# Seeding a PSUM bank by ScalarE for block product 2, and one more two-part group per layer, in a two-layer trunk

## The chip, the cores and the metric

The kernel runs on one core of one Trainium2 chip. The metric is the device time of one execution in microseconds; for the kernel before, the median of three runs is 967.45 us (967.29 to 968.33). The profile is of one further execution of the same program.

## The reference

The reference is a decoder trunk with two layers over 512 positions of 1,024 channels, batch 1, everything in float32. Each layer adds a mixer and then a gated convolutional FFN to the residual `h`. The change is in the FFNs alone:

```python
def gated_conv_ffn(x, w_gate, w_up, conv_w, conv_b, w_down):
    g = jnp.einsum('bsd,df->bsf', x, w_gate)
    g = causal_dwconv3(g, conv_w) + conv_b
    up = jnp.einsum('bsd,df->bsf', x, w_up)
    return jnp.einsum('bsf,fd->bsd', jax.nn.silu(g) * up, w_down)
...
        hn = rms_norm(h, norm_ffn[layer])
        h = h + gated_conv_ffn(hn, w_ffn_gate[layer], w_ffn_up[layer], conv_ffn[layer],
                               b_conv_ffn[layer], w_ffn_down[layer])
```

`w_gate` and `w_up` are 1,024 x 2,816 and `w_down` is 2,816 x 1,024; `causal_dwconv3` is a width-3 convolution along the positions.

## The kernel before

**Arithmetic.** A float32 product is computed from a high and a low part of each operand, both in the type fp32r: high times high, high times low, low times high. The high part is a ScalarE copy that rounds (`halves`, L831, or `parts`), the low part what is left, by a subtraction on VectorE (L832). Some low parts are made otherwise: ScalarE writes the negated rounded value (L144, L862) and a DMA on POOL's queue adds the source onto it (L146, L863).

**Groups.** The 2,816 hidden columns are 22 tiles of 128. In each layer the first two tiles are computed plainly (`direct`). The other twenty are ten groups of two tiles, f = 2, 4, ..., 20. `products` computes a group, for the gate (key "g") and for the up projection (key "u"), each as one 2 x 2 block product over two halves of the contraction, two column tiles and two halves of the positions, with seven block products instead of eight (Strassen-Winograd). So a group has 14 block products, of 128 columns of weights by 256 positions each, over four slices of 128 of the contraction.

**Narrow and wide.** A block product runs in one of two forms in `multiply`. The narrow form (L680) has three matmuls of 256 positions for each slice, twelve in all. The wide form (`both`, L670) gives one matmul the high and the low part of the positions side by side, 512 columns, for the high weights, and one of 256 columns for the low weights, eight matmuls in all. Its result lies in both halves of a PSUM bank, and the halves have to be added. `FIRST_WIDE` and `in_both` say which groups are wide. In layer 0, u is narrow before group 6; in group 6 g is wide and u wide in products 2, 5 and 3 alone; from group 8 on all is wide. In layer 1 it is the same two tiles earlier: mixed in group 4, all wide from group 6.

**Banks.** There are seven PSUM banks of 512 columns (`mm_bank`), taken in turn. By `BANK`, products 1, 6, 7 and 4 of one key accumulate in one bank "a" one after another, without clearing; products 5 and 3 share a bank "e"; product 2 has a bank "b" of its own. After a product, `after` reads the bank's running sum: a ScalarE copy to SBUF (L919, into `pads`, whose tiles are named rows, for g, or into `kept` for u), and VectorE adds of 256 columns (L907), one for each further half and each destination that the product contributes to (`onto`: product 2 is added where product 1 was put). A later product of the same bank can only be written once these reads are done.

**Order.** In `products` the fourteen block products are listed in an order by hand: g1, u1, g2, g5, g6, u5, u6, g7, u2, u7, g3, u3, g4, u4. After g3 and g4 the row is multiplied by the norm's factor (L931), convolved (`conv`: ScalarE L714, VectorE L716) and put through SiLU (L724); the products with u follow (L939 to L946). Between two groups stand matmuls of the down projection (`project` in layer 0, tiles d; `half_down` in layer 1, tiles dn), whose results VectorE adds to `h` (L317) or `y` (L1334).

**Preparation.** While one group runs, `prepare` makes the weights of the next: sums and differences of weight blocks on VectorE (s12g, s34g, s12u, s34u; L852 to L875) and their high and low parts (whi_..., wlo_...). In these groups the low parts of s12g, s34g and of the raw weights raw_g and raw_u go by the accumulating DMA, those of s12u and s34u by VectorE. A scheduler orders the instructions of each engine from the dependences, with priorities by the order of the source; each engine then runs its own list in order.

Of the kernel before, what the change touches and what calls it, by code (L numbers as in the profile page):

```python
# [31 lines left out]
def tile_trunk(ctx: ExitStack, tc: tile.TileContext, x, norm_mix, norm_ffn, final_norm,  # L32
# [3 lines left out]
    nc = tc.nc  # L36
# [9 lines left out]
    def mm_bank(name):  # L46
        return ps_mm.tile([P, 512], F32, tag="mm", name=name)
# [242 lines left out]
    def padded_tile():  # L290
        turn[0] += 1
        return padded[turn[0] % NPADDED]
# [352 lines left out]
    HALF = S // 2  # L645
# [1 line left out]
    PAIRS = [k for i in range(NP) for k in (i, i + NP)]  # L647

    FIRST_BY_DMA = 4
    FIRST_WIDE = ({"g": 6, "u": 8}, {"g": 4, "u": 6})  # L650

    BANK = {1: "a", 6: "a", 7: "a", 4: "a", 5: "e", 3: "e", 2: "b"}

# [37 lines left out]
    class Ffn:  # L691
# [195 lines left out]
        def products(self, f, stat):  # L887

            layer, ap, n = self.layer, self.ap, f"{self.layer}_{f}"
            banks = {"g": {}, "u": {}}  # L890
            kept = ap.tile([P, 3, HALF], F32, tag="kept", bufs=1, name=f"kept{n}")
            pads = [padded_tile() for _ in range(2)]
            lo, hi = slice(2, 2 + HALF), slice(2 + HALF, 2 + S)
            dst = {("g", 1): pads[0][:, lo], ("g", 6): pads[0][:, hi], ("g", 7): pads[1][:, hi],
                   ("g", 4): pads[1][:, lo]}
            dst.update({("u", product): kept[:, i, :] for i, product in enumerate((1, 6, 7))})
            onto = {2: 1, 7: 7, 3: 6}
            s = {}

            def in_both(key, product):  # L900
                first = FIRST_WIDE[layer]
                return f >= first[key] or f == first["g"] and product in (2, 5, 3)

            def add(d, bank, halves):
                ins = None
                for half in halves:
                    ins = nc.vector.tensor_tensor(d, bank[:, half * HALF : (half + 1) * HALF], d,  # L907
                                                  ALU.add)
                return ins

            def after(key, product, bank):
                halves = range(1 + in_both(key, product))
                if product in onto:
                    ins = add(dst[key, onto[product]], bank, halves)
                    if product == 7:
                        self.added[key] = ins
                elif (key, product) != ("u", 4):
                    d = dst[key, 7 if product == 5 else product]
                    nc.scalar.copy(d, bank[:, :HALF])  # L919
                    add(d, bank, halves[1:])  # L920

            for i, (key, product) in enumerate((
                    ("g", 1), ("u", 1), ("g", 2), ("g", 5), ("g", 6), ("u", 5), ("u", 6),
                    ("g", 7), ("u", 2), ("u", 7), ("g", 3), ("u", 3), ("g", 4), ("u", 4))):
                bank = self.multiply(banks[key], f"{key}{n}", product, stat[key, product],
                                     in_both(key, product), i % 2 == 1)
                after(key, product, bank)
                if (key, product) in (("g", 4), ("g", 3)):
                    j = product == 4
                    row = pads[j][:, 2:]  # L930
                    nc.vector.tensor_tensor(row, row, self.r, ALU.mult)  # L931
                    s[j] = self.silu(self.conv(pads[j], f + j), f + j)
                    if j and layer == 0:
                        nc.vector.tensor_tensor(s[1], s[1], self.r, ALU.mult)
            if layer == 0:
                nc.vector.tensor_tensor(kept[:, :2, :], kept[:, :2, :],
                                        self.r.rearrange("p (a b) -> p a b", a=2), ALU.mult)
            s0 = s[0].rearrange("p (a b) -> p a b", a=2)
            nc.vector.tensor_tensor(s0, kept[:, :2, :], s0, ALU.mult)  # L939
            nc.vector.tensor_tensor(s[1][:, HALF:], kept[:, 2, :], s[1][:, HALF:], ALU.mult)  # L940
            last = bank[:, :HALF]
            if in_both("u", 4):
                last = kept[:, 0, :]
                nc.scalar.copy(last, bank[:, :HALF])
                add(last, bank, (1,))
            nc.vector.tensor_tensor(s[1][:, :HALF], last, s[1][:, :HALF], ALU.mult)  # L946
            return [(f + 1, s[1]), (f, s[0])]
# [35 lines left out]
    def ffn0(norm):  # L983
        nonlocal prm1
        with tc.tile_pool(name="f0", bufs=1) as ap:
            def sums(kp):
                return [ap.tile([P, 2, HALF], F32R, name=f"t{i}_{kp}") for i in (2, 3)]

            ffn = Ffn(0, prm0, norm, ap, sums)
            def half_down(a, b, half):  # L990
                project(f"d0_{a}", w_ffn_down[0], ffn.acts, list(range(a, b)), None,
                        halves=(half,), tail=0)

            ffn.split_acts(ffn.steps(half_down))
            prm1 = params1(lambda ins: behind(ins, last_matmul[0]))
            nxt = Norm("m1", lambda k: prm1("mix", k))
            project("d0_last", w_ffn_down[0], ffn.acts, list(range(NF - 4, NF)), nxt)
            return nxt
# [547 lines left out]
    n = mixer0()  # L1546
    n = ffn0(n)
    n = mixer1(n)
# [31 lines left out]
```

## Time and profile before

| | |
|---|---|
| median of three runs | 967.45 us |
| the profiled execution | 968.03 us |
| its span | 966.3 us |
| TensorE matmul busy | 957.6 us (99%) |
| VectorE busy | 847.0 us (88%) |
| ScalarE busy | 620.7 us (64%) |
| GpSimd busy | 161.6 us (17%) |
| 256-column add, L907 | 0.42 us |
| 256-column copy, L919 | 0.36 us |

The page names the engines PE (TensorE's matmuls), PEld (its weight loads), DVE (VectorE), ACT (ScalarE), POOL (GpSimd) and SP (SyncE). A row of a timeline gives start, duration, engine, line, operation, output tile <- input tiles, and the shape; consecutive alike instructions are one row (x4). Ends of matmuls are modelled, so that the distance of two starts is the better measure of a matmul. Tiles g_12a and the like are the bank "a" of g's group 12. L numbers of the profile before are lines of the kernel before.

### The profile page before, as it was taken

The page shows a single profiled execution, that of the slowest core. Times are in us where ns is not written, and L with a number is a line of the kernel's source. Part 1 is how long each engine was busy: PE and PEld are TensorE (multiplying, and loading weights), DVE is VectorE, ACT ScalarE, POOL GpSimd, SP SyncE. Part 2 cuts the span into 40 slices and gives each one's busy share as a digit, 9 for nine tenths or more (in the row PEclk, how much of TensorE's full clock was granted, in tenths as well). Part 3 has the DMA queues.
Part 4 walks back from the last instruction along what each step waited for, and adds up shares of the span by engine and source line. Part 5 has one row for each costly group of instructions (what it writes and reads, how often), then busy time and mean ns, then how long its engine had stood idle before and what let it go on. Part 6 is the DMA issues. An engine that isn't in the chain of part 4 may idle for free.

```text
span 966.3 us, 14230 instructions
## 1 busy us (share of the span) xinstructions
PE 957.6 (99%) x5152; PEld 827.2 (86%) x5152; DVE 847.0 (88%) x1435; ACT 620.7 (64%) x940; POOL 161.6 (17%) x183
## 2 busy tenths in 40 slices
PE   9999999999999999999999999999999999999996
PEld 7888898998888888888888888989888888888885
DVE  5887988989899998998878689889998989889898
ACT  4624657766575565765487847787665667646775
POOL 2142224111011010110311002321111011100123
PEclk9999999999999999999999999999999999999999
DMA  7342345677777677774352323467767777667775
GB/s 253 134 151 87 66 135 128 170 188 188 175 174 174 154 174 196 164 184 132 131 153 87 109 88 88 140 137 182 183 150 191 196 175 174 177 151 196 196 152 142
DMA packets 95825, 150.45 MB, mean 156 GB/s; under 512 B 5284, under 2 KB 61580, under 8 KB 95756
## 3 DMA queue, kind: packets, MB, share of 16 engines
q1 hardware_dynamic: 78284, 98.69, 32.1%
q0 software_dynamic: 15696, 49.03, 28.1%
q10 hardware_dynamic: 1776, 1.84, 0.6%
q8 instruction: 40, 0.66, 0.3%
q14 instruction: 29, 0.24, 0.1%
HBM read 98.42 MB, written 2.10 MB: 104 GB/s over the span
## 4 chain that ended last, share of the span: by engine, by line
PE 99%; DVE 1%; issue 0%; POOLq 0%; DVEq 0%; POOL 0%; ACT 0%
PE d L159 3%; PE d L160 3%; PE dn L159 3%; PE dn L160 3%; PE dn L161 3%; PE d L161 3%; PE vu_a L1129 2%; PE gu L159 2%; PE gu L161 2%; PE gu L160 2%; PE u_2a L680 1%; PE g_2a L680 1%; PE u_4a L680 1%; PE u_20a L670 1%; PE u_18a L670 1%; PE u_12a L670 1%
## 5 line engine op out<-in xcount | busy, mean ns | idle before, releaser
L146 POOL DMA_DIRECT2D wlo_g<-raw_g x20 | 17.2, 860 | 310.0 <-DVE kept L907 142.2
L716 DVE SCALAR_TENSOR_TENSOR c<-rows,prm,c 128x512 f32<-128x512 f32 x88 | 65.4, 745 | 1.5 <-ACT c L714 1.5
L159 PE MATMUL d<-a_hi,whi_d 128*128 128x512 f32 x144 | 56.1, 389 | 0.0
L159 PE MATMUL dn<-whi_dn,a_hi 128*128 128x512 f32 x144 | 56.1, 389 | 0.0
L160 PE MATMUL d<-a_lo,whi_d 128*128 128x512 f32 x144 | 56.1, 389 | 0.0
L160 PE MATMUL dn<-wlo_dn,a_hi 128*128 128x512 f32 x144 | 56.0, 389 | 0.0
L161 PE MATMUL d<-a_hi,wlo_d 128*128 128x512 f32 x144 | 56.0, 389 | 0.0
L161 PE MATMUL dn<-whi_dn,a_lo 128*128 128x512 f32 x144 | 56.0, 389 | 0.0
L831 ACT ACTIVATE whi_a<-raw_g 128x512 fp32r<-128x512 f32 x20 | 12.6, 630 | 61.0 <-PE g_14e L670 8.5
L714 ACT ACTIVATE c<-rows,prm 128x512 f32<-128x512 f32 x44 | 31.4, 716 | 16.7 <-DVE rows L931 16.7
L1334 DVE SCALAR_TENSOR_TENSOR y<-dn,small,y 128x512 f32<-128x512 f32 x40 | 28.0, 749 | 7.8 <-PE dn L161 7.7
L724 ACT ACTIVATE s<-c,prm 128x512 f32<-128x512 f32 x44 | 31.4, 717 | 3.6 <-DVE c L716 3.6
L204 ACT ACTIVATE hg<-h,prm 128x512 fp32r<-128x512 f32 x24 | 17.3, 719 | 23.5 <-DVE h L317 17.0
L155 DVE TENSOR_TENSOR wlo_dn<-raw_dn,whi_dn 128x1024 fp32r<-128x1024 f32 x18 | 22.0, 1223 | 11.5 <-ACT whi_dn L154 11.5
L161 PEld LDWEIGHTS d<-a_hi,wlo_d 128*128 128x128 f32 x144 | 27.0, 188 | 5.7
L161 PEld LDWEIGHTS dn<-whi_dn,a_lo 128*128 128x128 f32 x144 | 27.0, 188 | 5.6
L160 PEld LDWEIGHTS dn<-wlo_dn,a_hi 128*128 128x128 f32 x144 | 27.0, 188 | 5.6
L159 PEld LDWEIGHTS dn<-whi_dn,a_hi 128*128 128x128 f32 x144 | 27.0, 188 | 5.6
L160 PEld LDWEIGHTS d<-a_lo,whi_d 128*128 128x128 f32 x144 | 27.1, 188 | 5.5
L159 PEld LDWEIGHTS d<-a_hi,whi_d 128*128 128x128 f32 x144 | 27.0, 188 | 5.5
L268 ACT ACTIVATE a_hi<-s 128x512 fp32r<-128x512 f32 x40 | 24.7, 625 | 10.5 <-PE d L161 9.4
L144 ACT ACTIVATE wlo_g<-raw_g 128x1024 fp32r<-128x1024 f32 x20 | 20.9, 1047 | 16.3 <-PE g_2e L680 7.6
(1271 smaller groups left out, 3377.7 us busy)
## 6 DMA issues: line engine op xcount, KB each, us to landing
raw_g<-in_w_ffn_gate_dram SPq DMA_DIRECT2D x40, 512.0 KB, 4.0
raw_u<-in_w_ffn_up_dram SPq DMA_DIRECT2D x40, 512.0 KB, 4.5
raw_dn<-in_w_ffn_down_dram SPq DMA_DIRECT2D x22, 512.0 KB, 4.7
wlo_g<-raw_g POOLq DMA_DIRECT2D x20, 512.0 KB, 4.5
wlo_u<-raw_u POOLq DMA_DIRECT2D x20, 512.0 KB, 6.0
raw_d<-in_w_ffn_down_dram SPq DMA_DIRECT2D x18, 512.0 KB, 4.1
wlo_s12g<-s12g POOLq DMA_DIRECT2D x18, 512.0 KB, 5.3
wlo_s34g<-s34g POOLq DMA_DIRECT2D x18, 512.0 KB, 5.2
```

The lines of the kernel that those rows point to most:

```text
L144: first = nc.scalar.activation(lo, raw, AF.Copy, scale=-1.0)
L155: behind(nc.vector.tensor_tensor(lo, raw, hi.bitcast(F32), ALU.subtract), after[0])
L159: nc.tensor.matmul(ps, lhs[0], rhs[0], start=start, stop=False)
L160: nc.tensor.matmul(ps, lhs[0], rhs[1], start=False, stop=False)
L161: nc.tensor.matmul(ps, lhs[1], rhs[0], start=False, stop=stop)
L268: nc.scalar.activation(hi, src, AF.Copy, scale=scale)
L670: last_matmul[0] = nc.tensor.matmul(ps if low else banks[at], left(kp)[low], right(kp)[0] if low else both(kp), start=first, stop=kp == NP ...
L680: nc.tensor.matmul(ps, l, r, start=first, stop=end, skip_group_check=True)
L714: nc.scalar.activation(c, t[:, 0:S], AF.Copy, scale=prm("cf", ft))
L716: self.last_conv = nc.vector.scalar_tensor_tensor(c, t[:, i : S + i], prm("cf", i * NF + ft), c, op0=ALU.mult, op1=ALU.add)
L724: self.last_silu = nc.scalar.activation(s, c, AF.Silu, bias=self.prm("bf", ft))
L1334: return nc.vector.scalar_tensor_tensor(dst, ps, ffn.cols[:, t : t + 1], dst, op0=ALU.mult, op1=ALU.add)
```

## The change

Two settings and the order of one product change, and `after` gets a second way.

- `FIRST_WIDE` moves one group earlier in both layers: the mixed group is now layer 0's group 4 and layer 1's group 2, and all groups behind are wide.
- From group 6 in layer 0 and group 4 in layer 1 (`FIRST_SEEDED`), product 1 is no longer read out to SBUF. Instead ScalarE copies its bank "a", both halves, to a new bank "b" (`seed`), and product 2 accumulates onto that bank, since `multiply` finds it there and does not clear it. Product 2's bank, now the sum of products 1 and 2, is then copied to product 1's destination and its second half added.
- g's copy is issued right after product 1 of g, u's after product 5 of u and ahead of that product's own copy.
- In the list of products, g5 now stands before g2.

```diff
@@ -647,7 +647,8 @@
-    FIRST_WIDE = ({"g": 6, "u": 8}, {"g": 4, "u": 6})
+    FIRST_WIDE = ({"g": 4, "u": 6}, {"g": 2, "u": 4})
+    FIRST_SEEDED = (6, 4)
@@ -908,9 +909,25 @@
+            def seeded(key):
+                return f >= FIRST_SEEDED[layer] and in_both(key, 1) == in_both(key, 2)
+
+            def seed(key):
+                b = banks[key]["b"] = mm_bank(f"{key}{n}b")
+                c = slice(0, HALF * (1 + in_both(key, 1)))
+                nc.scalar.copy(b[:, c], banks[key]["a"][:, c])
+
             def after(key, product, bank):
                 halves = range(1 + in_both(key, product))
-                if product in onto:
+                if seeded(key) and (key, product) in (("g", 1), ("u", 5)):
+                    seed(key)
+                if seeded(key) and product == 1:
+                    return
+                if seeded(key) and product == 2:
+                    d = dst[key, 1]
+                    nc.scalar.copy(d, bank[:, :HALF])
+                    add(d, bank, halves[1:])
+                elif product in onto:
                     ins = add(dst[key, onto[product]], bank, halves)
@@ -920,7 +937,7 @@
-                    ("g", 1), ("u", 1), ("g", 2), ("g", 5), ("g", 6), ("u", 5), ("u", 6),
+                    ("g", 1), ("u", 1), ("g", 5), ("g", 2), ("g", 6), ("u", 5), ("u", 6),
                     ("g", 7), ("u", 2), ("u", 7), ("g", 3), ("u", 3), ("g", 4), ("u", 4))):
```

## The prediction

> **What bounds the kernel now.** I read the page first, then the waits of TensorE, then the timeline of the groups that the diff touches.
>
> ```profile
> PE 957.6 (99%) x5152; PEld 827.2 (86%) x5152; DVE 847.0 (88%) x1435; ACT 620.7 (64%) x940; POOL 161.6 (17%) x183
> PEclk9999999999999999999999999999999999999999
> PE 99%; DVE 1%; issue 0%; POOLq 0%; DVEq 0%; POOL 0%; ACT 0%
> ...
> PE clock L61 <- DVE idle L56: 1.3, 1, 1.3
> ```
>
> TensorE is busy for 957.6 of 966.3 us, holds 99% of the chain that ends last, runs at full clock, and waits once, for 1.3 us, before the first matmul. So there is no wait in the FFNs to be won back: the change can gain only what it takes off TensorE's own work, and it loses whatever it makes TensorE wait. The next engine is VectorE at 88% on average; whether it has room must be read stage by stage.
>
> The profiled execution took 968.03 us, 0.58 above the median of 967.45. I form differences within its trace and add the sum to the median. By 0.2% of it, 1.93 us, a measurement of this kernel can about be told from no change; under 965.5 is faster, over 969.4 is slower.
>
> **TensorE's own work.** Rows of TensorE's timeline: start, duration, line, output; the first matmuls of a wide product, of a narrow one and of the next wide ones in layer 0's group 6; then the first matmul and the one that follows the group, for a group that is all narrow (layer 1, group 2), one that is mixed (layer 1, group 4) and one that is all wide (layer 0, group 12).
>
> ```profile
> 217.95 1.07 PE L670 MATMUL g_6a<-hg,whi_a 128*128 128x512 f32 x4
> 218.86 0.64 PE L670 MATMUL g_6a<-hg,wlo_a 128*128 128x256 f32 x4
> 219.33 0.40 PE L680 MATMUL u_6a<-hg,whi_a 128*128 128x256 f32 x2
> ...
> 220.77 1.09 PE L670 MATMUL g_6b<-hg,whi_g 128*128 128x512 f32 x4
> 222.17 0.64 PE L670 MATMUL g_6e<-t,wlo_s12g 128*128 128x256 f32 x4
> ...
> 645.24 0.40 PE L680 MATMUL g_2a<-hg,whi_a 128*128 128x256 f32 x2
> 665.39 0.40 PE L159 MATMUL dn<-whi_dn,a_hi 128*128 128x512 f32 x1
> 670.86 1.07 PE L670 MATMUL g_4a<-hg,whi_a 128*128 128x512 f32 x4
> 690.56 0.40 PE L159 MATMUL dn<-whi_dn,a_hi 128*128 128x512 f32 x1
> ...
> 309.52 1.07 PE L670 MATMUL g_12a<-hg,whi_a 128*128 128x512 f32 x4
> 329.07 0.39 PE L159 MATMUL d<-a_hi,whi_d 128*128 128x512 f32 x1
> ```
>
> A narrow product takes 220.77 − 219.33 = 1.44 us for 12 matmuls, a wide one 222.17 − 220.77 = 1.40 us for 8. Whole groups say it more exactly: 20.15 us all narrow, 19.70 mixed, 19.55 all wide. The diff moves each layer's mixed group one earlier: layer 0's group 4 and layer 1's group 2 go from narrow to mixed (−0.45 us each), the groups after them from mixed to wide (−0.15). Of 28 products that is 112 matmuls fewer, yet only −0.60 us per layer: **−1.2 us**, 0.12%. Faster by 0.2% is out of reach of this term alone.
>
> [...]
>
> **VectorE's adds and ScalarE's copies.** Two durations of the evacuation, and the one copy in the trace that has the seed's shape and reads a bank (it writes SBUF; no copy from bank to bank is there):
>
> ```profile
> L907 DVE TENSOR_TENSOR rows<-g_12a,rows x10: 415/418/426, 311.8 to 806.9; 128x256 f32<-128x256 f32 x10
> L919 ACT COPY rows<-g_12a x6: 353/356/375, 311.1 to 806.0; 128x256 f32<-128x256 f32 x6
> L1322 ACT COPY y<-hT x8: 566/586/608, 620.5 to 626.4; 128x512 f32<-128x512 f32 x8
> ```
>
> Every wide product costs one more add than a narrow one: +28 adds. Seeding takes two adds away for each key of the 17 seeded groups (product 1 gave one, product 2 two; now product 2 gives one), 68 in all. VectorE has 40 adds fewer, 17 us of 418 ns each, and since TensorE waits for none of them they buy nothing directly. ScalarE gets 34 seeds of 512 columns, and copies of product 2 where it copied product 1. At 64% it has room on average. Both depend on place.
>
> **The u seed, 17 times.** The seed of u reads product 1's bank, which u's product 6 goes on to fill, so product 6 now waits for it. In program order it stands behind g's product 6 copy, and that behind a weight split. From layer 0's group 12:
>
> ```profile
> 316.26 1.06 ACT L154 ACTIVATE whi_d<-raw_d 128x1024 fp32r<-128x1024 f32 x1 [0.53 <-PE g_12a L670]
> 317.23 0.35 ACT L919 COPY rows<-g_12a 128x256 f32<-128x256 f32 x1
> ...
> 316.01 0.64 PE L670 MATMUL g_12a<-t,wlo_s12g 128*128 128x256 f32 x4
> 317.90 1.07 PE L670 MATMUL u_12a<-t,whi_s12u 128*128 128x512 f32 x4
> ...
> 655.98 0.36 ACT L919 COPY kept<-u_2a 128x256 f32<-128x256 f32 x1
> 656.23 0.63 ACT L831 ACTIVATE whi_a<-raw_u 128x512 fp32r<-128x512 f32 x1
> ```
>
> The split's buffer is freed by the high half of g's product 6, 0.25 us after its last issue (316.01 to 316.26), so ScalarE can't go earlier. The copy starts at 317.23; the engine goes on 0.25 us after a copy's start (655.98 to 656.23): the seed starts at 317.48 and ends at 318.07 by the nearest row's 586 ns. Product 6 starts at 317.90; the changed program puts one 512-column matmul of g's product 3 ahead of it (227 ns, a quarter of a wide product's high half, 0.91 us from 217.95 to 218.86), so it is due at 318.13. That leaves 0.06 us for the hand-over. From TensorE to ScalarE it takes up to the 0.25 above; I take 0.1, so product 6 comes 0.04 us late, 17 times: **+0.7 us**. The bounds: at 0.356 us (the 256-column copy) nothing; at 1.05 us (the 1,024-column split) 0.5 late, +8.5. 586 ns is nearest in shape and source. The g seed has no such trouble: it reads a bank done at 1.4 us into the group, and product 2 now starts at 4.2, 2.8 later, which covers its 0.59 and a split before it.
>
> [...]
>
> **VectorE where the adds come before the relief.** Layer 0's group 4 and layer 1's group 2 get 10 adds more each (7 of g, 3 of u) and are not seeded. Busy time by stretch, each about from one group's start to the next's (length, then PE, PEld, DVE, ACT, POOL); the second of each pair is the group behind:
>
> ```profile
> 192.03:217.65 25.62, 25.62 (x194) 24.66 (x193) 22.78 (x39) 18.32 (x28) 3.62 (x5) 1.00 0.81 195
> 217.65:248.33 30.68, 30.68 (x178) 26.94 (x177) 27.88 (x52) 20.30 (x29) 4.30 (x5) 1.00 0.80 193
> 644.93:670.55 25.62, 25.62 (x194) 24.66 (x193) 23.95 (x39) 20.65 (x32) 3.44 (x4) 1.00 0.64 159
> 670.55:695.72 25.17, 25.17 (x154) 22.53 (x153) 23.89 (x45) 17.99 (x27) 3.47 (x5) 1.00 0.79 186
> ```
>
> Adds follow each other every 0.33 us (657.93, 658.53 and 658.86 below: an add from 658.53 to the next start at 658.86), so 10 take 3.3. Layer 0's stretch then holds 26.1 us in 25.2, 0.9 too many, and group 6 behind it has 2.8 to spare: I take nothing there, with 0.9 as the other bound. Layer 1's holds 27.3 in 25.2, 2.1 too many, and the next has only 1.3. What slips is the preparation of group 4's weights:
>
> ```profile
> 657.93 0.68 DVE L852 TENSOR_TENSOR s12g<-raw_g,raw_g 128x512 f32<-128x512 f32 x1
> 658.53 0.42 DVE L907 TENSOR_TENSOR kept<-u_2b,kept 128x256 f32<-128x256 f32 x1
> 658.86 0.68 DVE L854 TENSOR_TENSOR s12g<-s12g,raw_g 128x512 f32<-128x512 f32 x1
> 665.69 0.74 DVE L716 SCALAR_TENSOR_TENSOR c<-rows,prm,c 128x512 f32<-128x512 f32 x1
> 671.34 1.40 DVE L1334 SCALAR_TENSOR_TENSOR y<-dn,small,y 128x512 f32<-128x512 f32 x2
> 672.66 1.22 DVE L832 TENSOR_TENSOR wlo_s12u<-s12u,whi_s12u 128x1024 fp32r<-128x1024 f32 x1
> 667.77 1.05 ACT L862 ACTIVATE wlo_s34g<-s34g 128x1024 fp32r<-128x1024 f32 x1
> 668.72 1.04 ACT L864 ACTIVATE whi_s34g<-s34g 128x1024 fp32r<-128x1024 f32 x1
> 677.87 0.64 PE L670 MATMUL u_4e<-t,wlo_s12u 128*128 128x256 f32 x4
> DMA to landing us min/median/max: 4.8/5.3/8.2
> ```
>
> In the changed order s12g's second half stands behind g's first convolution steps (about 666 us, in place of 658.86), so the copy that starts its accumulating DMA on POOL's queue comes at about 667.4 and the DMA at 668.7; landing takes 4.8 to 8.2 (wlo_s12g), to 673.5 to 676.9. g's product 5, now third, needs it 3.7 us into group 4, which starts at 670.41 (670.86 less 0.45): 674.1. At the median it lands just in time. s34g stands behind the last y adds (free at 672.66 now); its two 0.6 us steps end near 673.75. Then ScalarE does four splits in order, 0.95 us apart (667.77 to 668.72): wlo_s34g, whi_s34g, wlo_u and whi_s12u, which ends at 677.7; VectorE's wlo_s12u (1.22) ends at 679.0. u's product 5 begins with that tile: today at 677.87, 7.01 into the group, there after five wide products at 677.4. **+1.6 us** of wait. If the y adds come 0.9 earlier, it is 0.7; if the slow landing rules, 676.9 − 674.1 = 2.8. What is late next is g's product 7 (wlo_s34g's DMA, issued near 675.5) and u's product 2; both have moved by the same wait.
>
> **Sum.** −1.2 + 0.7 + 1.6 = +1.1: 967.45 + 1.1 = 968.5 us.
>
> **The rivals.**
> A: the seed's price decides, and it is dear. The mechanism is ScalarE's queue before u's product 6: a seed of d us comes d − 0.55 late (317.48 + d + 0.1 against 318.13). From 0.64 us the kernel is slower by 0.2%; at 0.65 us it is 967.45 − 1.2 + 1.6 + 17 × 0.1 = 969.55, at 0.8 us 17 × 0.25 = 4.3 and 972.1. For it: the margin of 0.06 us and no row for bank to bank. Against: 608 is the largest of eight, and the changed order may start ScalarE's split earlier. Chance 0.33.
> B: the pure saving. ScalarE's seeds fit, and VectorE's idle 1.7 us in layer 1's group 2, plus reordering, takes up the adds: 967.45 − 1.2 = 966.25. For it: TensorE waits nowhere now. Against: the order of s34g and s12u above. Chance 0.17.
> C: faster by over 0.2% wants 1.94 us, 0.7 more than the matmuls give; 40 fewer adds could give it only if TensorE waited for VectorE, and the row of waits shows none: 965.4. Chance 0.04.
> The forecast, one wait in layer 1 and seeds about in time (966.8 to 969.4): 0.46.
> That the change does not do what it says: order and counts move as told, so the chance is nil that nothing moves; that the scheduler undoes it in time is B.
>
> **How the numbers follow.** Faster is C, 0.04; slower is A plus a few hundredths of the forecast (a landing at its slowest, 2.8 for 1.6, gives 969.7), 0.37; the rest is 0.59. The forecast's own range is 966.8 to 969.4. The 8-in-10 range reaches from B's 966.1 to A's 972.0; it leaves out C, the last bit of B, and a seed above 0.8 us.
>
> **What would show it.** Groups of 19.70 us at layer 0's group 4 and layer 1's group 2, and 19.55 after them, confirm the saving. A row of TensorE waiting at u's product 5 (bank e) in layer 1's group 4 for wlo_s12u, near 1.6 us, confirms the slip; a wait at g's product 5 instead points at the DMA. The seed's rows give its price; TensorE's waits at u's product 6 for ScalarE, 17 times, give A. Wrong would be: waits at g's product 2 (the g seed), or at product 7 for an add.

## The result, and the profile after

The changed kernel takes 970.06 us (median of 11 runs, 969.39 to 971.42); the kernel before, run beside it, 967.89 us (11 runs). The ratio is 1.0024, with a 95% interval of 1.0016 to 1.0032: slower by 2.2 us. The forecast was 968.5 us with a range of 966.1 to 972.0; no change was given 0.59, slower 0.37. The range holds the time, but the forecast's own case (966.8 to 969.4) does not, and slower was not the likeliest case. Both losses that it named are there; a third, in layer 1's group 6, it did not name.

The page of the changed kernel, and under it TensorE's waits and three of the waits of its weight loads (PEld; total, times, longest):

```profile
PE 957.5 (99%) x5040; PEld 820.4 (85%) x5040; DVE 834.9 (86%) x1395; ACT 637.3 (66%) x976; POOL 161.6 (17%) x183
PE 94%; DVE 3%; ACT 1%; DMA 0%; issue 0%; POOLq 0%; DVEq 0%; POOL 0%
...
PE u_4e L671 <- DVE wlo_s12u L833: 1.5, 1, 1.5
PE clock L61 <- DVE idle L56: 1.3, 1, 1.3
PE u_6e L671 <- DVE wlo_s12u L833: 0.5, 1, 0.5
PE z L443 <- ACT hg L411: 0.3, 1, 0.3
...
PEld u_16a L671 <- ACT u_16b L918: 0.5, 2, 0.3
PEld u_10a L671 <- ACT u_10b L918: 0.4, 2, 0.2
PEld u_6a L671 <- ACT u_6b L918: 0.3, 1, 0.3
```

TensorE has 112 matmuls fewer, 5,040 for 5,152, yet its busy time is the same, since a busy row is stretched where it waits inside (the row of u's product 6 in group 12, below, takes 1.19 us for 1.07). VectorE is 12 us less busy and ScalarE 17 us more. In the chain that ended last VectorE and ScalarE now hold 3% and 1%; before, TensorE had 99% and VectorE 1%. Two of the new waits are those that the prediction named: u's product 5 (bank e) in layer 1's group 4, for wlo_s12u, and u's product 6 (bank a), whose weight loads stand behind the seed in every seeded group but layer 1's 4 and 6. The third, u's product 5 in layer 1's group 6, it did not name. The 0.3 us at z lie 6 us into the program, which the change does not touch.

A group's time is read from TensorE's timeline, from its first matmul to the first of the next stage (us):

| group | before | changed |
|---|---|---|
| layer 0, group 4 | 20.15 | 19.73 |
| layer 0, group 6 | 19.77 | 19.70 |
| layer 0, group 12 / 14 | 19.55 / 19.57 | 19.68 / 19.58 |
| layer 0, all ten | 196.97 | 196.99 |
| layer 1, group 2 | 20.15 | 19.77 |
| layer 1, group 4 | 19.70 | 21.32 |
| layer 1, group 6 | 19.60 | 20.28 |
| layer 1, group 12 / 14 | 19.55 / 19.55 | 19.65 / 19.63 |
| layer 1, all ten | 196.29 | 198.83 |

The two groups that lose narrow products win their 0.4 us each. In layer 0 the seeded groups give all of it back: groups 8 to 20 are 0.01 to 0.13 us longer than before, and group 6, now all wide, takes 19.70 in place of 19.55. Layer 1 loses 2.5 us on balance. The span grew by 2.2 us (966.3 to 968.5); 0.3 us in the other direction lie ahead of layer 0's group 2, which starts at 166.4 in place of 166.7.

**The seed.** Its rows, and its place in layer 0's group 12 (timelines of ScalarE, TensorE and the weight loads); at the end, product 6 of u in group 14:

```profile
L918 ACT COPY g_12b<-g_12a x2: 570/570/570, 310.5 to 790.8; 128x512 f32<-128x512 f32 x2
L918 ACT COPY u_12b<-u_12a x2: 591/592/592, 316.8 to 797.1; 128x512 f32<-128x512 f32 x2
...
316.55 0.35 ACT L936 COPY rows<-g_12a 128x256 f32<-128x256 f32 x1
316.80 0.59 ACT L918 COPY u_12b<-u_12a 128x512 f32<-128x512 f32 x1
...
317.21 0.40 PE L671 MATMUL g_12e<-hg,whi_s34g 128*128 128x512 f32 x1
317.45 1.19 PE L671 MATMUL u_12a<-t,whi_s12u 128*128 128x512 f32 x4
...
316.99 0.19 PEld L671 LDWEIGHTS g_12e<-hg,whi_s34g 128*128 128x128 f32 x1
317.44 0.77 PEld L671 LDWEIGHTS u_12a<-t,whi_s12u 128*128 128x128 f32 x4 [0.27 <-ACT u_12b L918]
...
347.78 1.12 PE L671 MATMUL u_14a<-t,whi_s12u 128*128 128x512 f32 x4
347.69 0.76 PEld L671 LDWEIGHTS u_14a<-t,whi_s12u 128*128 128x128 f32 x4 [0.19 <-ACT u_14b L918]
```

The seed ends at 317.39, before product 6 is due at 317.44. It is late all the same, because its weight load waits for the seed too (0.27 us, to 317.44), where the load before it runs 0.2 us ahead of its matmul (316.99 for 317.21). The matmul then starts at its time by the model but the four take 1.19 us for the 1.07 of an undisturbed row. What a group loses follows the wait of this weight load: from group 8 on, waits of 0.19 to 0.20 us go with 0.01 to 0.03 us, 0.22 us with 0.06 to 0.08, and 0.27 us with 0.10 to 0.13. In group 14 no matmul of g's product 3 stands ahead, and the load still starts 0.09 us before its matmul (347.69 for 347.78).

The 34 bank-to-bank copies of the changed kernel take 570 to 606 ns (g's 570 to 583, u's 590 to 606), within the 566 to 608 of the copy to SBUF.

**Layer 1's group 4.** The chain that ends in the 1.5 us, from VectorE's, ScalarE's and TensorE's timelines; the last row is s34g in the kernel before:

```profile
666.45 0.69 DVE L855 TENSOR_TENSOR s12g<-s12g,raw_g 128x512 f32<-128x512 f32 x1
672.28 0.68 DVE L874 TENSOR_TENSOR s34g<-raw_g 128x512 f32<-128x512 f32 x1
677.53 1.23 DVE L833 TENSOR_TENSOR wlo_s12u<-s12u,whi_s12u 128x1024 fp32r<-128x1024 f32 x1 [1.56 <-ACT whi_s12u L832]
...
667.25 1.05 ACT L863 ACTIVATE wlo_s12g<-s12g 128x1024 fp32r<-128x1024 f32 x1
673.60 1.06 ACT L863 ACTIVATE wlo_s34g<-s34g 128x1024 fp32r<-128x1024 f32 x1 [0.71 <-DVE s34g L876]
676.46 1.04 ACT L832 ACTIVATE whi_s12u<-s12u 128x1024 fp32r<-128x1024 f32 x1
...
676.68 0.63 PE L671 MATMUL g_4a<-t,wlo_s12g 128*128 128x256 f32 x4
678.81 0.74 PE L671 MATMUL u_4e<-t,wlo_s12u 128*128 128x256 f32 x4 [1.49 <-DVE wlo_s12u L833]
...
659.46 0.68 DVE L873 TENSOR_TENSOR s34g<-raw_g 128x512 f32<-128x512 f32 x1
```

s12g's second half starts at 666.45 (658.86 before), s34g at 672.28 behind the y adds (659.46 before), whi_s12u ends at 677.50 and wlo_s12u at 678.76: u's product 5 is 1.49 us late.

### The profile page after: what moved, and what is told of

It is laid out like the page before. It is cut to its first block, busy times and chain, and to the rows that moved or that the text cites. A ratio compares the mean times of both kernels' runs of the same rounds, so it can differ in the third digit from the quotient of the medians.

```text
span 968.5 us, 13973 instructions
## 1 busy us (share of the span) xinstructions
PE 957.5 (99%) x5040; PEld 820.4 (85%) x5040; DVE 834.9 (86%) x1395; ACT 637.3 (66%) x976; POOL 161.6 (17%) x183
## 4 chain that ended last, share of the span: by engine, by line
PE 94%; DVE 3%; ACT 1%; DMA 0%; issue 0%; POOLq 0%; DVEq 0%; POOL 0%
PE d L160 3%; PE d L161 3%; PE d L159 3%; PE dn L159 3%; PE dn L160 3%; PE dn L161 3%; PE vu_a L1146 2%; PE gu L159 2%; PE gu L161 2%; PE gu L160 2%; PE u_8a L671 1%; PE u_12a L671 1%; PE u_16a L671 1%; PE u_20a L671 1%; PE u_14a L671 1%; PE u_18a L671 1%
## 5 line engine op out<-in xcount | busy, mean ns | idle before, releaser
L833 DVE TENSOR_TENSOR wlo_s34u<-s12u,whi_s34u 128x1024 fp32r<-128x1024 f32 x20 | 24.5, 1224 | 14.2 <-ACT whi_s34u L832 14.2
L155 DVE TENSOR_TENSOR wlo_d<-raw_d,whi_d 128x1024 fp32r<-128x1024 f32 x18 | 22.0, 1222 | 10.9 <-ACT whi_d L154 10.9
```

What stands on the lines that cost most here:

```text
L155: behind(nc.vector.tensor_tensor(lo, raw, hi.bitcast(F32), ALU.subtract), after[0])
L833: nc.vector.tensor_tensor(lo, src, hi.bitcast(F32), ALU.subtract)
```

## The experiments

All of them are compared with the kernel before, run beside them (967.8 to 968.0 us). The theory: the ten adds more in layer 1's group 2 make groups 4 and 6 wait, and the seed of u is handed over a little late 17 times. The rivals put the loss on the seeds alone, on the new product order, or on ScalarE's load.

### 1. Layer 1's wide groups put back

```diff
-    FIRST_WIDE = ({"g": 4, "u": 6}, {"g": 2, "u": 4})
+    FIRST_WIDE = ({"g": 4, "u": 6}, {"g": 4, "u": 6})
```

> The changed kernel with layer 1's wide groups put back (mixed in group 4, wide from 6), all else kept. Theory: the 2.0 us of wait at u's product 5 in layer 1's groups 4 (1.49) and 6 (0.46) come from the 10 adds more in layer 1's group 2. Then they are gone: 970.06 - 2.0 + 0.6 (layer 1's saving given up), about 968.6 us, and no wait for wlo_s12u. Rival: the new product order and the seeds, which are still there, make g4 wait; then the wait stays and the time is about 970.6.

Measured: 968.71 us, ratio 1.0007 (0.9998 to 1.0016). Group 4 of layer 1 takes 19.70 us and group 6 also 19.70; the wait for wlo_s12u is not there. The late weights belong to layer 1's shift.

### 2. The wide groups alone

```diff
-    FIRST_WIDE = ({"g": 6, "u": 8}, {"g": 4, "u": 6})
+    FIRST_WIDE = ({"g": 4, "u": 6}, {"g": 2, "u": 4})
```

(in the kernel before: no seeds)

> The kernel before with the new wide groups alone: no seeds, old product order. Theory: the wait in layer 1's group 4 is there without any seed, 1.2 to 2 us, and layer 0 and the groups from 8 on run as before (19.55 us): 967.89 - 1.2 + 1.5 to 2.5, about 968.2 to 969.2 us. Rival (the seeds on ScalarE delay the weights): no wait, 966.7 us.

Measured: 982.36 us, ratio 1.0137 (1.0118 to 1.0156), 13 us past the upper end. Layer 1's groups 4, 6, 8 and 10 take 20.70, 30.72, 20.87 and 20.20 us, layer 0's group 10 20.34. TensorE's longest waits, then rows of TensorE and VectorE in layer 1's group 6, and a stretch of that group with the clock that TensorE was granted (third figure from the end):

```profile
PE g_6a L670 <- DVE rows L907: 3.7, 1, 3.7
PE g_6e L670 <- DMA wlo_s12g<-s12g: 2.5, 1, 2.5
PE u_8a L670 <- DVE kept L907: 1.1, 1, 1.1
PE g_10a L670 <- DVE rows L907: 0.9, 2, 0.5
...
698.88 1.09 PE L670 MATMUL u_6a<-hg,whi_a 128*128 128x512 f32 x4
703.66 0.77 PE L670 MATMUL g_6a<-t,whi_s12g 128*128 128x512 f32 x1 [3.69 <-DVE rows L907]
704.41 2.08 PE L670 MATMUL g_6b<-hg,whi_g 128*128 128x512 f32 x4
...
715.87 1.08 PE L670 MATMUL u_6e<-t,whi_s12u 128*128 128x512 f32 x4
...
703.10 0.42 DVE L907 TENSOR_TENSOR rows<-g_6a,rows 128x256 f32<-128x256 f32 x1
...
702.00:714.00 12.00, 7.83 (x21) 6.01 (x22) 5.22 (x10) 7.46 (x9) 2.58 (x3) 0.50 0.93 210
```

Without seeds VectorE does not catch up. The longest wait, 3.7 us, is product 6 of g in group 6 (its weights are s12g), and it waits for the add of product 1 from the same bank, which VectorE reaches only at 703.10; the weight load of the same product waits 4.1 us for whi_s12g. Seeding takes the read of that add away, so it can help in two ways, by fewer adds and by one dependence less; this run does not part them. So seeding does buy TensorE something here, against the prediction's "they buy nothing directly": with it the backlog of group 2 ends in group 6.

Not all of the 14.4 us is waiting. In group 6 TensorE's granted clock is 0.50 in the stretch from 702.00 to 714.00 us, and four matmuls of 512 columns take 2.08 us at 704.41, where they took 1.09 at 698.88 and take 1.08 from 715.87. By a difference, 30.72 − 19.55 − 3.7 − 2.5, some 5 us are an estimate of what that cost. The five executions spread from 978.4 to 983.1 us.

### 3. The seeds alone

```diff
-    FIRST_WIDE = ({"g": 4, "u": 6}, {"g": 2, "u": 4})
+    FIRST_WIDE = ({"g": 6, "u": 8}, {"g": 4, "u": 6})
```

> The changed kernel with the old wide groups: seeds and product order alone. Theory: layer 1 waits nowhere for wlo_s12u, and each seeded group of u is 0.03 to 0.13 us longer than 19.55, about 1.1 us in all: 967.89 + 1.1, about 969.0 us. Rival (seeds are free, the whole loss is the wait in layer 1): 967.9 us. Rival (the seeds cause the wait in layer 1): 970.5 us or more.

Measured: 969.93 us, ratio 1.0021 (1.0012 to 1.0030), 0.9 above the theory. The groups from 8 on take 19.59 to 19.68 us as expected, but two do not: layer 0's group 6 takes 20.21 us (19.77 before), with a wait of 0.3 us at product 7 of g for an add, and layer 1's group 8 19.96, where the weight load of u's product 6 waits 0.6 us for the seed. None of the three forecasts met this. Seeds without the shift lose 1.9 us, the shift without seeds 14.4, both together 2.2: the two parts can't be priced apart and added.

### 4. The seed of u right after product 1 of u

```diff
-                if seeded(key) and (key, product) in (("g", 1), ("u", 5)):
+                if seeded(key) and (key, product) in (("g", 1), ("u", 1)):
```

> The changed kernel with u's seed issued right after product 1 of u, seven microseconds before product 6 of u needs the bank. Theory: the groups from 8 on return to 19.55 us (now 19.58 to 19.68) since the hand-over to product 6 was all that the seed cost, and the wait in layer 1's groups 4 and 6 stays: 970.06 - 1.1, about 969.0 us. Rival (a seed costs because ScalarE or PSUM is shared, wherever it stands): groups stay at 19.58 to 19.68 and the time at 970.1.

Measured: 975.54 us (974.48 to 977.18 in four executions), ratio 1.0080 (1.0066 to 1.0094). Half of the theory holds: layer 0's groups 6 to 20 and layer 1's from 12 take 19.54 us, each of them. In layer 0's group 12, TensorE and ScalarE:

```profile
311.77 0.57 ACT L918 COPY u_12b<-u_12a 128x512 f32<-128x512 f32 x1 [0.78 <-PE u_12a L671]
...
316.23 1.09 PE L671 MATMUL u_12e<-t,whi_s12u 128*128 128x512 f32 x4
317.16 1.07 PE L671 MATMUL u_12a<-t,whi_s12u 128*128 128x512 f32 x4
```

The seed is written from 311.77, product 6 follows product 5 at 317.16, 5.4 us later (not the seven of the expectation), and its row is back at 1.07. A seed costs nothing where there is time to hand it over. But layer 1's groups 4, 6 and 8 take 20.65, 23.66 and 22.00 us:

```profile
PE g_8b L671 <- ACT g_8b L918: 2.1, 1, 2.1
PE g_6e L671 <- DMA wlo_s34g<-s34g: 1.4, 1, 1.4
PE g_6e L671 <- ACT whi_s34g L865: 1.0, 1, 1.0
PE u_6a L671 <- ACT whi_s12u L832: 0.7, 1, 0.7
```

The late preparation now goes on to s34g in group 6 and, in group 8, to the seed of g itself, which ScalarE reaches only behind a row of weight splits (734.79 us, 4.4 us into the group).

### 5. The early seed of u, with layer 1's wide groups put back

```diff
-    FIRST_WIDE = ({"g": 4, "u": 6}, {"g": 2, "u": 4})
+    FIRST_WIDE = ({"g": 4, "u": 6}, {"g": 4, "u": 6})
...
-                if seeded(key) and (key, product) in (("g", 1), ("u", 5)):
+                if seeded(key) and (key, product) in (("g", 1), ("u", 1)):
```

> Layer 1's wide groups put back and u's seed right after product 1 of u, in both layers. Layer 0 should run at 19.54 us in every group from 6 on, as with the early seed before. It tells what made layer 1 worse with the early seed (groups 6 and 8 at 23.7 and 22.0 us). Theory: VectorE's overflow from group 2, which the early seed only made worse; without it layer 1 has no wait: 968.0 - 0.6, about 967.4 us. Rival: the early seed itself is too early for layer 1, where ScalarE is late at the start of a group; then groups 6 and 8 wait again and the time is 970 us or more.

Measured: 966.90 us, ratio 0.9991 (0.9982 to 1.0000). Layer 1 runs at 19.54 us in every group from 8 on, with no wait in it: the early seed does no harm there by itself, and the waits of run 4 came from the backlog of group 2. It is the fastest median of all, and its interval just reaches no change. In the profiled execution layer 0's group 10 takes 20.24 us, with a wait of 0.3 us for g's seed; the other runs with this layer 0 do not show it.

### 6. The seed of u written twice

```diff
-                nc.scalar.copy(b[:, c], banks[key]["a"][:, c])
+                for _ in range(1 + (key == "u")):
+                    nc.scalar.copy(b[:, c], banks[key]["a"][:, c])
```

> The changed kernel with the seed of u written twice (the same copy again), that of g once. Theory: product 6 of u waits for that copy, so each of the 17 groups grows by about the pace of one such copy, 0.5 us: 970.06 + 8 to 9, about 978.5 us, with waits at u's product 6. Rival (the 0.03 to 0.13 us per group are not the hand-over of the seed): within 1 us of 970.

Measured: 977.50 us, ratio 1.0100 (1.0086 to 1.0113), 7.4 us more than with one. TensorE's waits:

```profile
PE u_4e L671 <- DVE wlo_s12u L833: 1.5, 1, 1.5
PE u_18a L671 <- ACT u_18b L919: 0.9, 1, 0.9
PE u_16a L671 <- DVE kept L908: 0.9, 1, 0.9
PE u_10a L671 <- ACT u_10b L919: 0.9, 1, 0.9
```

Product 6 of u does wait for the seed, so ScalarE's queue at that place is on the path. The growth is not even, though: layer 0's groups from 6 on take 19.8 to 21.4 us, layer 1's from group 8 on 19.76 to 19.82. In layer 0's groups 10, 14 and 18 another ScalarE copy stands between the two, and product 6 waits 0.9 us; in groups 8 and 16 product 4 of u waits for an add (0.2 and 0.9 us), which the theory did not have. So the total is near the theory's 8 to 9 us partly by luck.

### 7. g seeded in the first mixed groups too

```diff
-    FIRST_SEEDED = (6, 4)
+    FIRST_SEEDED = (4, 2)
```

> The changed kernel with g seeded in the first mixed group of each layer too (layer 0 group 4, layer 1 group 2; u is not, its product 1 being narrow there): two adds fewer in layer 1's group 2, and the sums s12g and s34g of group 4 come ahead of the convolution again in VectorE's order. Theory: the waits for wlo_s12u in layer 1's groups 4 and 6 (1.49 and 0.46 us) come from that order and go away: 970.06 - 2.0, about 968.1 us. Rival (VectorE's total is what counts): two adds are 0.7 us of it, the wait in group 4 shrinks by 0.7 and the time is about 969.4 us.

Measured: 970.31 us, ratio 1.0025 (1.0016 to 1.0035). The wait for wlo_s12u is gone, as the theory said (groups 4 and 6 of layer 1 take 19.77 and 19.90 us), but the time is no lower, and the rival's 969.4 is missed too. The wait has moved into group 2 itself, 21.11 us, and layer 0's group 4 takes 20.23:

```profile
PE g_2a L671 <- DVE rows L908: 1.1, 1, 1.1
PE g_4a L671 <- DVE rows L908: 0.3, 1, 0.3
```

With s12g and s34g back in front, the adds come late for product 7 of g. VectorE's list holds too much there in both orders; the order chose who waited. The output of this kernel and the next is 2.2% off the reference (see the last section); the amount of work is as intended.

### 8. The same in layer 1 alone, and the early seed of u in layer 0

```diff
-    FIRST_SEEDED = (6, 4)
+    FIRST_SEEDED = (6, 2)
...
-                if seeded(key) and (key, product) in (("g", 1), ("u", 5)):
+                if seeded(key) and (key, product) in (("g", 1), ("u", 5 if layer else 1)):
```

> The changed kernel with u's seed right after product 1 of u in layer 0 alone, and with g seeded in layer 1's group 2. Theory: layer 0 gains its 0.6 us in full (groups at 19.54), layer 1 loses only the hand-over of its u seeds (some 0.7 us): 968.0 - 1.2 + 0.7, about 967.5 us, between the kernel before and a little under it. Rival (VectorE's total in layer 1): 1.3 us more, 968.8 us.

Measured: 969.10 us, ratio 1.0011 (1.0003 to 1.0020), nearer the rival's 968.8 than the theory's 967.5. Layer 0 takes 19.54 us from group 6 on and 19.70 in group 4; layer 1's group 2 again takes 21.12 us.

### 9. Without the ten adds

```diff
-                halves = range(1 + in_both(key, product))
+                halves = range(1 + (in_both(key, product) and (layer, f) != (1, 2)))
```

> The changed kernel without the 10 adds of second bank halves in layer 1's group 2 (so the low-part products of that group are missing from its sums); its matmuls stay as changed. Theory: those 10 adds alone make groups 4 and 6 wait: the two waits for wlo_s12u (1.49 and 0.46) and what hangs on them go, 970.06 - 2.2, about 967.9 us, with group 2 at 19.77 and group 4 near 19.7 us. Rival (the product order or the seeds in group 4 share the blame): a wait of over 0.5 us at u's product 5 stays, 968.5 us or more.

Measured: 968.27 us, ratio 1.0005 (0.9997 to 1.0014), 1.8 less than the changed kernel. Its matmuls, seeds and product order are the changed kernel's; group 4 of layer 1 takes 19.62 us and group 6 19.92, and one wait of a matmul is left in the whole kernel:

```profile
PE clock L61 <- DVE idle L56: 1.3, 1, 1.3
```

So the ten adds are the cause of both waits. The rest of group 6 is not theirs: there the weight load of u's product 6 waits 0.5 us for the seed.

### 10. Half of layer 1's shift

```diff
-    FIRST_WIDE = ({"g": 4, "u": 6}, {"g": 2, "u": 4})
+    FIRST_WIDE = ({"g": 4, "u": 6}, {"g": 4, "u": 4})
...
-                if seeded(key) and (key, product) in (("g", 1), ("u", 5)):
+                if seeded(key) and (key, product) in (("g", 1), ("u", 1)):
```

> Seed of u right after product 1 of u; layer 0 as changed; in layer 1 group 2 narrow and groups 4 on all wide, so that layer 1 takes only the second half of its shift, 4 products of u in group 4. Theory: group 4 can bear its 4 adds, since its seeds take 4 away; layer 1 gains 0.15 us and waits nowhere, layer 0 gains 0.6: 967.9 - 0.75 - 0.2, about 967.0 us. Rival (any add more in layer 1 before the seeded groups makes it wait): 968 us or more.

Measured: 967.03 us, ratio 0.9993 (0.9985 to 1.0002). Layer 0 wins what it should, 19.54 us in each group from 6 on. Layer 1's groups 4 and 6 take 19.76 and 19.82 us for 19.70 and 19.60 before, and no matmul is listed as waiting there. The weight loads are: 0.4 us for the seed of g in group 4, 0.2 for it in group 6 and 0.2 for an add. VectorE's adds are no reason in group 4, 16 there as before, four more for the wide products and four fewer by the seeds. So, as far as the waits show, what the four wide products win is lost to seeds of g that come late, in group 4 behind ScalarE's splits at the group's start.

### 11. Layer 1 without seeds

```diff
-    FIRST_WIDE = ({"g": 4, "u": 6}, {"g": 2, "u": 4})
-    FIRST_SEEDED = (6, 4)
+    FIRST_WIDE = ({"g": 4, "u": 6}, {"g": 4, "u": 6})
+    FIRST_SEEDED = (6, 99)
...
-                if seeded(key) and (key, product) in (("g", 1), ("u", 5)):
+                if seeded(key) and (key, product) in (("g", 1), ("u", 1)):
```

> Layer 0 as changed with u's seed right after product 1 of u; layer 1 without seeds and with its old wide groups. Theory: layer 1's early seeds neither gain nor lose, since VectorE's relief there buys nothing: the same 966.9 us as with them, within 0.4. Rival (the relief of 36 adds in layer 1 is what made that kernel faster than the one before): 967.5 us or more.

Measured: 967.30 us, ratio 0.9995 (0.9987 to 1.0004). Between the theory's 966.9 and the rival's 967.5; runs 5, 10 and 11 can't be told apart from each other by their intervals, and hardly from the kernel before. By the groups, layer 1 takes 196.36 us in this run and 196.22 in run 5.

### 12. The old product order

```diff
-                    ("g", 1), ("u", 1), ("g", 5), ("g", 2), ("g", 6), ("u", 5), ("u", 6),
+                    ("g", 1), ("u", 1), ("g", 2), ("g", 5), ("g", 6), ("u", 5), ("u", 6),
```

> The changed kernel with g2 put back ahead of g5. Theory: the seed of g is ready 1.9 us or so into the group and product 2 of g would start at 2.8, so steady groups stay at 19.58 to 19.68; the waits at u's product 5 in layer 1's groups 4 and 6 stay, since the order of VectorE's list there is the same: about 970 us. Rival (moving g5 ahead of g2 brought the wait, by asking for s12g earlier): the waits shrink by 0.5 us and more, 969.3 us or less.

Measured: 970.02 us, ratio 1.0024 (1.0014 to 1.0035), the changed kernel's own. The waits at u's product 5 stay:

```profile
PE u_4e L671 <- DVE wlo_s12u L833: 1.5, 1, 1.5
PE u_6e L671 <- DVE wlo_s12u L833: 0.3, 1, 0.3
```

So the product order is not a cause of that wait or of the loss.

## Why the prediction was right or wrong

- **TensorE's bound and the −1.2 us.** Right. With the early seed layer 0 shows it clean: group 4 at 19.71 us and group 6 at 19.54, where they took 20.15 and 19.77, with all the other groups at 19.54.
- **The u seed, +0.7 us.** The right place, half the size. The price was right (592 ns for 586), and so was the start behind the copy (0.25 us, 316.55 to 316.80). The step that failed is the hand-over, "I take 0.1": it was argued for the matmul, and it is the weight load, 0.2 us ahead of the matmul, that waits for the seed (0.19 to 0.29 us in the rows of PEld). The working also put a matmul of g's product 3 ahead of product 6 in every group; groups 10, 14 and 18 have none in layer 0. Against the 19.55 us of an all-wide group, layer 0's groups from 6 on are 0.71 us longer in sum and layer 1's from 8 on 0.63: +1.3. Run 4 shows that this goes when the seed is early, run 6 that it grows with the seed.
- **The wait in layer 1's group 4, +1.6 us.** Right in place, cause and size: 1.49 us, for wlo_s12u, through the s34g and whi_s12u named. The DMA of s12g was no bound: it landed 4.6 us after its issue at 668.59, and the matmuls that read wlo_s12g start at 673.89 without a wait.
- **"What is late next".** Wrong. The working looked for it behind the wait in the same group, at g's product 7 and u's product 2. It was group 6 (0.46 us at its own wlo_s12u; the group 0.68 longer than before). The sum of layer 1's stretches said so: 2.1 us too many with 1.3 to spare behind leaves 0.8 for the group after, and that was not carried on. Run 9, without the ten adds, still takes 19.92 us there, with a late seed of u, so the backlog accounts for about half of group 6's 0.73 us over 19.55.
- **"They buy nothing directly" of the 40 adds.** Right where layer 1 is not widened: run 11, without seeds there, is within the intervals of run 5. Wrong beside the shift: run 2 loses 14.4 us without the seeds, some 5 of it at the halved clock, and seeding takes from TensorE's path an add that it there waits 3.7 us for. The working asked only whether TensorE waits for VectorE today.
- **Layer 0's group 4, nothing.** Right: 19.73 us.
- **The sum.** By groups: saving 0.42 + 0.22 in layer 0 and 0.38 + 0.15 in layer 1, together −1.2; the seeds of the 15 groups above +1.3; groups 4 and 6 of layer 1, over the 19.55 of an all-wide group, +1.8 and +0.7; less 0.1 that the kernel before already lost: +2.6. Ahead of the FFN 0.3 less, where group 2 of layer 0 starts anywhere from 165.8 to 166.7 us in the profiles of this study: near the measured +2.2. The forecast's +1.1 lacked 0.6 for the seeds and about 0.9 for group 6 and the rest of group 4.
- **The rivals and the range.** Slower came, in part at rival A's place, but not for its reason: it wanted a seed of 0.64 us or more, and the seed took 0.57 to 0.61. The range holds 970.06 because its upper end was set by that dear seed; in this it was lucky. 0.4 us of the 1.6 between forecast and result are the kernel before itself, 967.89 beside the changed one for the 967.45 that the sum started from.

## What to carry to other kernels

Where the bound engine waits for nothing, a change that trades its work for work on an engine at 88% must be judged in the stage where the work lands and in the ones behind: carry the backlog from stretch to stretch until it is gone, since what waits depends on the late engine's order. Here the one other order tried moved the wait from group 4 into group 2 and gained nothing. In this kernel a dependence on a fresh result had to be met at the weight load, 0.2 us ahead of the matmul. Issuing the copy as soon as its source was ready (5 us earlier in the group) made it free in the steady groups; where ScalarE was behind at the start of a group, the other seed, g's, waited instead (runs 4, 5 and 10). Two parts of one change may need each other: their prices, 1.9 and 14.4 us alone (the latter with some 5 us at a halved clock), were 2.2 together.

## What was not expected of the hardware

In the changed kernel a ScalarE copy from bank to bank takes 570 to 606 ns for 512 columns (537 to 583 in run 4), about as long as one to SBUF in the kernel before (566 to 608). A weight load waited for the seed of the bank that its matmul was to write (run 4 and the changed kernel, group 12: no wait with the early seed, 0.27 us with the late one). In run 2 TensorE ran dry at 699.97 us (698.88 + 1.09) and waited until 703.66; the granted clock was 0.50 in the stretch from 702.00 to 714.00, and 0.990 in the mean of the whole span. What set it off is not shown: with a wait of 1.5 us in the changed kernel the clock was 1.00 over that group, and with one of 2.1 us in run 4 it was 0.998 in the mean, as in the kernel before. In the groups seeded by the changed kernel product 2 added onto what ScalarE had written, as the output of run 12, with the same seeds, shows. In runs 7 and 8, where g of layer 1's group 2 was seeded too, the output moved by 2.2%; no run here shows the cause.
